# Relative-position biases of a two-block transformer: moved from the feed-forward stage into the set-up, with fewer, larger stores

## The chip, the core and the metric

The kernel runs on one core of a Trainium2 chip. The metric is the device time of one execution in microseconds; the time of a kernel is the median of its runs. TensorE is called PE, its weight loads PEld, VectorE DVE, ScalarE ACT, GpSimd POOL and SyncE SP. A "q" behind an engine's name stands for its instruction queue where it issues a transfer.

## The reference

Two blocks of two layers each on x (256 tokens x 1024, float32). The first block has, in each layer, a feed-forward part, three kinds of attention and a second feed-forward part, each behind a norm that is scaled and shifted by vectors made from a condition c. The change touches the biases of the sliding-window attention: a table of 32 buckets x 6 heads, looked up by the bucket of the distance between two positions.

```python
def modulate(x, g, shift, scale):
    return rms_norm(x, g) * (1.0 + scale[:, None, :]) + shift[:, None, :]
...
    cond = jax.nn.silu(c)
    for l in range(DEPTH):
        mod = cond @ w_mod[l] + b_mod[l]
        sh1, sc1, g1, sh2, sc2, g2, sh3, sc3, g3 = jnp.split(mod, 9, axis=-1)
        h = modulate(x, norm_g[l, 0], sh1, sc1)
        x = x + 0.5 * g1[:, None, :] * swiglu(h, w_ffn1_gu[l], w_ffn1_down[l])
...
def swa_attention(q, k, v, pos, sinks, rel_table):
...
    rel = pos.reshape(B, nb, WINDOW)[..., :, None] - band(pos)[..., None, :]
    bias = rel_table[t5_bucket(rel)].astype(jnp.float32)
```

The bias of a distance depends only on how many of 32 bucket edges the distance has reached, so it can be written as a sum of the table's steps over the edges reached.

## The kernel before

**Matmuls.** A float32 weight tile (`raw`, 128x1024, four 128-row chunks of 256 columns, 512 KB) is split into a high part (`whi`, ACT) and a low part (`wlo`, DVE); the operand likewise (`oph`, `opl`). A product is three matmuls: high x high (L218), low x high (L231), high x low (L235). PE runs its queue in order, as every engine does.

**The set-up** (`setup`) is a schedule written out by hand: the instructions go to the engines' queues in the order of the code. SP issues x in two halves, c, b_mod and norm_g, then the eight row blocks of w_mod for the scale vector "sc" (L437). PE transposes x (`take_x`, L771), ACT copies it to the chip and squares it, DVE adds the squares (`ssq`, L657, six adds). Then PE multiplies the condition by the eight row blocks (`gv`, L447, `self.next_step`). Behind the third of them it makes the row sums (L575), from which DVE takes the inverse root (`nv` ... `nry`, L584 to L540); behind the seventh it spreads them over the partitions (`dg`, L592 on DVE, L596 on PE). Then `fill_operand` makes `oph` and `opl` with the scale vector.

**The held products.** `held_parts` computes the first ten half blocks of `w_ffn1_gu` in the set-up, in a loop over b of 0 to 9. Block b is 24 matmuls. Behind an odd b below 8 DVE scales the two results (`held`, L351). Then come the steps of the shift vector "sh" (`gv`, as many as `SH_HELD` says), then `held.high(b + 2)` (ACT, L326) and `held.low(b + 2)` (DVE, L332): parts are made two blocks ahead. `LOADS` says what SP loads ahead of each block; one small load goes out with each letter.

**The biases.** `bias_loads` prepares ten small loads: `posk` (all positions to each partition), four of `posq`, four of the table, and `posi`. After block 5 (`REL_AT`) `rel_bias` makes `thr` (query position less edge, L1013, L1014), `kf` (key positions, L1016), the steps of the table (a matmul with `step`, L1018, then `tabs` and three bfloat16 parts `tabp`), and the first two of eight pieces `ge`: for four queries and 384 keys, whether each edge is reached (two instructions, L1035, on DVE). The rest is six "looks", each a function in the list `self.later`. A look is twelve bfloat16 matmuls (32 columns x 512, L1050) into one PSUM bank, one or two further pieces of `ge` (two buffers), an eviction `bev` by ACT (L1054) and four stores by ACT's queue (48 KB each, L1058), 24 stores in all, to `bias_scratch` in DRAM, which the attention reads much later.

**Behind the set-up.** In the feed-forward stage a framework schedules by priorities. `pace` pops one function of `self.later` at every third weight block (`T5_EVERY`) from the sixteenth (`T5_WAIT`): the six looks, then six functions `rest` (other vectors and the masks) and the rope tables. SP issues the stage's weight loads (L186) at the end of the set-up.

Of the kernel before, what the change touches and what calls it, by code (L numbers as in the profile page):

```python
# [9 lines left out]
F32 = mybir.dt.float32  # L10
F32R = mybir.dt.float32r
BF16 = mybir.dt.bfloat16
# [6 lines left out]
P = 128  # L19
# [26 lines left out]
SMALL = 1  # L46
LOADS = ("w", "sw", "sw", "sw", "sw", "ssw", "ssw", "w", "", "")
T5_HELD = (0,)*10
# [6 lines left out]
REL_AT = 5  # L55
# [76 lines left out]
class Net:  # L132
# [640 lines left out]
    def setup(self, tmp):  # L773
# [41 lines left out]
        with self.tc.manual_schedule():  # L815
# [12 lines left out]
            small_loads = self.bias_loads(tmp)  # L828
# [4 lines left out]
            nc.scalar.dma_start(early, A["cst"][:, o0:o1])  # L833
            self.x = self.t(self.xp, [P, 8, S], F32, "x")
# [5 lines left out]
            finish_1()  # L840
            for n in range(4):
                self.take_x(xn, n)
            self.preload(8)
            wgu, kp = A["w_ffn1_gu"][0], kept.enter_context(self.tc.tile_pool(name="kept", bufs=1))
# [20 lines left out]
            for b in range(10):  # L865
                for x in LOADS[b]:
# [5 lines left out]
                    for f in small_loads[:SMALL]:  # L872
                        f()
                    small_loads = small_loads[SMALL:]
# [22 lines left out]
        def rest(n):  # L897
# [12 lines left out]
            else:  # L910
                mk = self.t(tmp, [P, 512], F32, "bev", 2)
# [11 lines left out]
        self.later += [lambda n=n: rest(n) for n in range(6)] + [lambda: self.rope_tables(tmp)]  # L923
# [66 lines left out]
    def bias_loads(self, pool):  # L990
# [5 lines left out]
        self.posi = self.t(pool, [P, 2], I32, "posi")  # L996
        self.tab = self.t(pool, [P, 32], F32, "tab")
# [7 lines left out]
        pairs.append((self.posi, pos[0].rearrange("(t p) -> p t", p=P)))  # L1005
        return [lambda o=o, i=i: nc.sync.dma_start(o, i) for o, i in pairs]

    def rel_bias(self, pool):
        nc, A = self.nc, self.A
        self.scratch = nc.dram_tensor("bias_scratch", (6, P, 384), F32).ap()  # L1010
        posq, posk, tab = self.posq, self.posk, self.tab
        thr = self.t(pool, [P, 2, 32], F32, "thr")
        nc.vector.tensor_copy(thr, posq)  # L1013
        nc.vector.tensor_scalar(out=thr, in0=thr, scalar1=self.edges, scalar2=None, op0=ALU.subtract)  # L1014
        kf = self.t(pool, [P, S], F32, "kf")
        nc.vector.tensor_copy(kf, posk)  # L1016
        ps = self.sm()
        nc.tensor.matmul(ps[:, 0:32], lhsT=self.step, rhs=tab, start=True, stop=True)  # L1018
        steps = self.t(pool, [P, 32], F32, "tabs")
        nc.scalar.activation(out=steps, in_=ps[:, 0:32], func=AF.Copy)  # L1020
        parts, rest = [], steps
        for n in range(3):
            part = self.t(pool, [P, 32], BF16, "tabp%d" % n)
            nc.vector.tensor_copy(part, rest)
            parts.append(part)
            if n < 2:
                left = self.t(pool, [P, 32], F32, "tabr%d" % n)
                nc.vector.tensor_tensor(out=left, in0=rest, in1=part, op=ALU.subtract)
                rest = left
        ge = {}  # L1030

        def reached(piece):
            t = ge[piece] = self.t(pool, [P, 4, 384], BF16, "ge", 2)
            for a, w, blk in ((0, P, 0), (P, S, 1)):
                nc.vector.tensor_tensor(  # L1035
                    out=t[:, :, a : a + w],
# [4 lines left out]
        def look(n):  # L1041

            ps = self.sm()
            for t in range(4):
                piece, j = divmod(4 * n + t, 3)
                if piece not in ge:
                    reached(piece)
# [735 lines left out]
```

## Time and profile before

| | us |
|---|---|
| median of 3 runs | 1905.13 |
| lowest, highest run | 1897.05, 1905.39 |
| the profiled execution's own time | 1893.67 |
| its span | 1891.9 |
| mean granted clock over the span | 0.99 |

The span is the time from the first to the last instruction of the profiled execution. A row of a timeline gives start and length of a group of like instructions in us, the engine, line and operation, out<-in, and in brackets how long the engine was idle before it and what ended that. "PEclk" is the granted TensorE clock as a share of full speed.

### The profile page before, as it was taken

The numbers are of one execution on the slowest core, as the hardware profiler recorded it, in microseconds if no ns is written. First come the engines' busy times: TensorE is split into PE (matmuls) and PEld (weight loads), VectorE is DVE, ScalarE is ACT, GpSimd is POOL, SyncE is SP. The second block draws the span as 40 slices with busy tenths as digits, with TensorE's granted clock in tenths as the row PEclk, the third lists the DMA queues.
The fourth block names the chain that finished last, engine by engine and source line by source line (L and its number), as shares of the span: only waits on it lengthen the run. The fifth ranks groups of instructions, "written<-read, shape, count | busy, mean of one in ns | idle before, by whom it ended". The sixth has DMA issues, their size and how long they took to land.

```text
span 1891.9 us, 37147 instructions
## 1 busy us (share of the span) xinstructions
PE 1839.9 (97%) x15125; PEld 1736.0 (92%) x15125; DVE 1371.3 (72%) x2171; ACT 960.2 (51%) x1527; POOL 0.2 (0%) x4
## 2 busy tenths in 40 slices
PE   7999999999999999999999999999999999999998
PEld 5899996899999999968999988999999888999998
DVE  4897576698669765768986696679865777577554
ACT  3444475554445444756544454546444545455443
POOL 0000000000000000000000000000000000000000
PEclk8999999999999999999999999999999999999999
DMA  9698545789857963458798477578984585775550
GB/s 319 195 331 288 187 141 191 267 279 378 283 178 274 319 230 118 135 190 296 249 340 269 157 250 235 195 233 281 337 267 147 189 295 178 248 252 186 195 191 23
DMA packets 229447, 440.72 MB, mean 233 GB/s; under 512 B 15590, under 2 KB 79708, under 8 KB 229276
## 3 DMA queue, kind: packets, MB, share of 16 engines
q1 hardware_dynamic: 227740, 436.96, 68.0%
q8 instruction: 118, 1.93, 0.4%
q10 hardware_dynamic: 1536, 1.39, 0.2%
q14 instruction: 53, 0.43, 0.1%
HBM read 436.06 MB, written 2.23 MB: 232 GB/s over the span
## 4 chain that ended last, share of the span: by engine, by line
PE 87%; DVE 6%; DMA 3%; ACT 2%; issue 1%; SPq 0%; DVEq 0%; ACTq 0%
PE mm L218 24%; PE mm L235 23%; PE mm L231 23%; DVE wlo L198 2%; PE mm L262 2%; PE mm L265 2%; PE mm L263 2%; PE gv L447 2%; PE sm L771 1%; ACT whi L197 1%; DMA raw<-in_w_ffn_gu_dram 1%; PE mm L771 1%; PE gv L481 1%; DMA rawx<-in_w_mod_dram 1%; DMA raw<-in_w_mod_dram 1%
## 5 line engine op out<-in xcount | busy, mean ns | idle before, releaser
L218 PE MATMUL mm<-oph,whi 128*128 128x256 f32 (+1 forms) x3072 | 786.3, 282 | 13.3 <-DVE dly L302 4.9
L231 PE MATMUL mm<-opl,whi 128*128 128x256 f32 (+1 forms) x3072 | 780.0, 280 | 0.1
L197 ACT ACTIVATE whi<-raw 128x1024 fp32r<-128x1024 f32 (+2 forms) x408 | 426.2, 1047 | 455.4 <-PE mm L231 352.1
L198 DVE TENSOR_TENSOR wlo<-raw,whi 128x1024 fp32r<-128x1024 f32 (+2 forms) x408 | 489.8, 1208 | 176.5 <-ACT whi L197 168.5
L218 PEld LDWEIGHTS mm<-oph,whi 128*128 128x128 f32 x3072 | 582.5, 190 | 30.1 <-issue 10.3
L231 PEld LDWEIGHTS mm<-opl,whi 128*128 128x128 f32 x3072 | 582.6, 190 | 2.2 <-issue 0.9
L235 PE MATMUL mm<-oph,wlo 128*128 128x256 f32 (+1 forms) x3072 | 574.8, 280 | 8.6 <-DVE wlo L198 8.4
L235 PEld LDWEIGHTS mm<-oph,wlo 128*128 128x128 f32 x3072 | 453.9, 190 | 12.2 <-DVE wlo L198 11.1
L197 ACT ACTIVATE whi<-rawx 128x1024 fp32r<-128x1024 f32 x160 | 170.1, 1064 | 193.8 <-PE mm L231 159.0
L218 PE MATMUL mm<-ah,whi 128*128 128x256 f32 x1056 | 268.1, 278 | 0.0
L231 PE MATMUL mm<-al,whi 128*128 128x256 f32 x1056 | 267.0, 277 | 0.0
L198 DVE TENSOR_TENSOR wlo<-rawx,whi 128x1024 fp32r<-128x1024 f32 x160 | 194.8, 1223 | 91.3 <-ACT whi L197 90.6
L454 DVE SCALAR_TENSOR_TENSOR acc<-raw,silc,acc 128x1024 f32<-128x1024 f32 x119 | 152.5, 1283 | 77.9 <-DMA raw<-in_w_ada_dram 60.4
L235 PE MATMUL mm<-ah,wlo 128*128 128x256 f32 x1056 | 206.8, 277 | 0.7 <-DVE wlo L198 0.7
L218 PEld LDWEIGHTS mm<-ah,whi 128*128 128x128 f32 x1056 | 198.4, 188 | 3.0 <-issue 2.5
L231 PEld LDWEIGHTS mm<-al,whi 128*128 128x128 f32 x1056 | 198.5, 188 | 0.0
L235 PEld LDWEIGHTS mm<-ah,wlo 128*128 128x128 f32 x1056 | 159.5, 188 | 1.1 <-DVE wlo L198 1.1
L262 PE MATMUL mm<-whi,oph 128*128 128x512 f32 (+2 forms) x192 | 73.9, 388 | 0.3 <-ACT oph L640 0.2
L263 PE MATMUL mm<-whi,opl 128*128 128x512 f32 (+2 forms) x192 | 73.0, 380 | 0.0
L454 DVE SCALAR_TENSOR_TENSOR acc<-rawx,silc,acc 128x1024 f32<-128x1024 f32 x42 | 53.9, 1283 | 18.3 <-DMA rawx<-in_w_ada_dram 9.3
L698 ACT ACTIVATE ah<-sil 128x512 fp32r<-128x512 f32 x66 | 40.3, 624 | 37.0 <-DVE sil L760 29.7
L265 PE MATMUL mm<-wlo,oph 128*128 128x512 f32 (+2 forms) x192 | 56.6, 378 | 0.0
(374 smaller groups left out, 1660.3 us busy)
## 6 DMA issues: line engine op xcount, KB each, us to landing
raw<-in_w_mod_dram SPq DMA_DIRECT2D x119, 512.0 KB
raw<-in_w_ffn_gu_dram SPq DMA_DIRECT2D x104, 512.0 KB
raw<-in_w_in_dram SPq DMA_DIRECT2D x104, 512.0 KB
raw<-in_w_ada_dram SPq DMA_DIRECT2D x75, 512.0 KB
rawx<-in_w_ffn_gu_dram SPq DMA_DIRECT2D x64, 512.0 KB
raw<-in_w_ffn_down_dram SPq DMA_DIRECT2D x54, 512.0 KB
raw<-in_w_ffn_in_dram SPq DMA_DIRECT2D x48, 512.0 KB
rawx<-in_w_ffn_in_dram SPq DMA_DIRECT2D x40, 512.0 KB
```

The source lines that it names most:

```text
L197: nc.scalar.activation(out=whi[:, :tot], in_=src, func=AF.Copy)
L198: nc.vector.tensor_tensor(out=wlo[:, :tot], in0=src, in1=whi[:, :tot].bitcast(F32), op=ALU.subtract)
L218: i0 = nc.tensor.matmul(o, lhsT=whi[:, k, cs], rhs=xhi[:, kop0 + k, :ncol], start=zero and (opener or not shared), stop=False, **kw)
L231: nc.tensor.matmul(o, lhsT=whi[:, k, cs], rhs=xlo[:, kop0 + k, :ncol], start=False, stop=False, **kw)
L235: nc.tensor.matmul(o, lhsT=wlo[:, k, cs], rhs=xhi[:, kop0 + k, :ncol], start=False, stop=last and k == nk - 1, **kw)
L262: nc.tensor.matmul(o, lhsT=xhi[:, kop0 + k, ts], rhs=whi[:, k, cols], start=first and k == 0, stop=False)
L263: nc.tensor.matmul(o, lhsT=xlo[:, kop0 + k, ts], rhs=whi[:, k, cols], start=False, stop=False)
L265: nc.tensor.matmul(o, lhsT=xhi[:, kop0 + k, ts], rhs=wlo[:, k, cols], start=False, stop=last and k == nk - 1)
L447: nc.tensor.matmul(acc[32 * g : 32 * g + 32, 0:S], lhsT=self.cond[cond][1][:, k, :], rhs=row[:, g * S : (g + 1) * S], start=k == 0, stop=k ...
L454: nc.vector.scalar_tensor_tensor(out=acc, in0=row, scalar=self.cond[cond][0][:, k : k + 1], in1=acc, op0=ALU.mult, op1=ALU.add)
L698: nc.scalar.activation(out=hi, in_=src, func=AF.Copy)
L771: self.nc.tensor.transpose(out, in_, self.ident[:n, :n])
```

## The change

The small loads go to ACT's queue at the very start, nine of them; the table is loaded once per group of 32 partitions into `buckets` and copied into a matmul operand by four DVE copies. `thr`, `kf` and `ge` 0 and 1 stand among the x steps, the step-table matmul ahead of the first `gv`; two looks stand among the row blocks of the scale vector, four in the loop of the held products, each further piece behind `held.low`. The six evictions are kept in six buffers, and SP stores them, 256 KB each, at the end of the loop, with two unused heads as padding (8 heads in `bias_scratch`). `self.later` holds only the six `rest` and the rope tables. The mask's staging tile has a buffer of its own.

```diff
-SMALL = 1
-T5_HELD = (0,)*10
+LOOK_AT = (3, 5)
-REL_AT = 5
...
-            small_loads = self.bias_loads(tmp)
+            self.posi = self.t(tmp, [P, 2], I32, "posi")
+            kp = kept.enter_context(self.tc.tile_pool(name="kept", bufs=1))
...
             nc.scalar.dma_start(early, A["cst"][:, o0:o1])
+            self.bias_loads(kp)
+            bias = self.rel_bias(kp)
...
             finish_1()
+            bias.distances()
+            bias.reached(0)
             for n in range(4):
                 self.take_x(xn, n)
+                if n == 1:
+                    bias.reached(1)
+            bias.table()
             self.preload(8)
...
                 if n == RS_AT:
                     rs = self.row_rs(self.mm)
+                if n == LOOK_AT[0]:
+                    bias.look(0)
+                    bias.reached(2)
+                if n == LOOK_AT[1]:
+                    bias.look(1)
+                    bias.reached(3)
                 if n == RB_AT:
                     self.rb = self.row_scale(self.mm, rs)
...
                     held.high(b + 2)
                     held.low(b + 2)
-                if b == REL_AT:
-                    self.later = self.rel_bias(tmp)
-                for _ in range(T5_HELD[b]):
-                    self.later.pop(0)()
+                if b == 1:
+                    bias.look(2)
+                if 2 <= b <= 5:
+                    bias.reached(b + 2)
+                if 3 <= b <= 5:
+                    bias.look(b)
+            nc.sync.dma_start(self.posi, A["positions"][0].rearrange("(t p) -> p t", p=P))
+            for _ in range(6):
+                bias.store()
...
-                mk = self.t(tmp, [P, 512], F32, "bev", 2)
+                mk = self.t(tmp, [P, 512], F32, "mk")
...
-        self.later += [lambda n=n: rest(n) for n in range(6)] + [lambda: self.rope_tables(tmp)]
+        self.later = [lambda n=n: rest(n) for n in range(6)] + [lambda: self.rope_tables(tmp)]
...
-            pairs.append((self.tab[rows, 6 * g : 6 * g + 6], A["rel_bias"]))
+            pairs.append((self.buckets[rows], A["rel_bias"]))
+        for o, i in pairs:
+            nc.scalar.dma_start(o, i)
...
+            def table(self):
+
+                for g in range(4):
+                    rows = slice(32 * g, 32 * g + 32)
+                    nc.vector.tensor_copy(net.tab[rows, 0:6, g], net.buckets[rows])
+                ps = net.sm()
+                nc.tensor.matmul(
+                    ps[:, 0:32], lhsT=net.step, rhs=net.tab.rearrange("p h g -> p (h g)"), start=True, stop=True
+                )
...
+                ev = net.t(pool, [P, 512], F32, "bev", 6)
+                nc.scalar.activation(out=ev, in_=ps, func=AF.Copy)
+                evs.append((n, ev))
+
+            def store(self):
+                n, ev = evs.pop(0)
+                to = net.scratch.rearrange("h (g r) k -> (h g) (r k)", g=4)[:, 2048 * n : 2048 * n + 2048]
+                nc.sync.dma_start(to.rearrange("m (t c) -> t m c", t=4), ev)
```

In the changed kernel lines up to some 820 are 2 lower than before (L447 is L445, L332 is L330, L351 is L349, L575 is L573, L596 is L594, L657 is L655); the looks' matmuls are at L1073, `ge` at L1060, the step-table matmul at L1043, the stores at L1081.

In the rows of order below, a number behind a name only tells buffers apart.

PE between the transposes of x (`mm<-ident`) and the fourth row block of the scale vector, before:

```order
L771 MATMUL mm_153<-ident_75,raw_77 128x128
L771 MATMUL mm_153<-ident_75,raw_78 128x128
L447 MATMUL gv_181<-raw_100,repc_112 32x256 x4
L447 MATMUL gv_181<-raw_102,repc_112 32x256 x4
L447 MATMUL gv_181<-raw_104,repc_112 32x256 x4
L575 MATMUL mm_195<-ones_81,ssq_124 128x1 x2
L575 MATMUL mm_195<-ones_81,sq_162 128x1 x2
L447 MATMUL gv_181<-raw_164,repc_112 32x256 x4
```

and after:

```order
L769 MATMUL mm_177<-ident_75,raw_77 128x128
L769 MATMUL mm_177<-ident_75,raw_78 128x128
L1043 MATMUL sm_192<-tab_99,cst_4_80 128x32
L445 MATMUL gv_220<-raw_115,repc_127 32x256 x4
L445 MATMUL gv_220<-raw_117,repc_127 32x256 x4
L445 MATMUL gv_220<-raw_119,repc_127 32x256 x4
L573 MATMUL mm_234<-ones_81,ssq_145 128x1 x2
L573 MATMUL mm_234<-ones_81,sq_186 128x1 x2
L445 MATMUL gv_220<-raw_206,repc_127 32x256 x4
L1073 LDWEIGHTS tabp_44_196
L1073 MATMUL sm_263<-ge_136,tabp_44_196 32x512
```

The step-table matmul `sm<-tab,cst` now stands between the transposes and the first `gv`. The first look's matmuls (`sm<-ge,tabp`, 24 rows with their weight loads) follow the fourth row block, the second look's follow the sixth, ahead of `L594`.

DVE in the same place, from the last two of the six adds of squares into the steps of the inverse root, before:

```order
L657 TENSOR_TENSOR ssq_124<-ssq_124,sq_150 128x256
L657 TENSOR_TENSOR ssq_124<-ssq_124,sq_159 128x256
L584 TENSOR_SCALAR nv_194<-mm_195 128x2
L513 TENSOR_SCALAR nri_201<-nv_194 128x2
L515 TENSOR_SCALAR nry_203<-nri_201 128x2
L521 TENSOR_SCALAR nrh_206<-nv_194 128x2
L536 TENSOR_SCALAR nrt_205<-nry_203,nrh_206 128x1 x2
```

and after, from `kf` to the four copies:

```order
L1035 CAST kf_111<-posk_97 128x256
L1060 TENSOR_TENSOR ge_136<-thr_110,kf_111 128x4x128
L1060 TENSOR_TENSOR ge_136<-thr_110,kf_111 128x4x256
L655 TENSOR_TENSOR ssq_145<-ssq_145,sq_147 128x256
L655 TENSOR_TENSOR ssq_145<-ssq_145,sq_156 128x256
L655 TENSOR_TENSOR ssq_145<-ssq_145,sq_159 128x256
L1060 TENSOR_TENSOR ge_162<-thr_110,kf_111 128x4x128
L1060 TENSOR_TENSOR ge_162<-thr_110,kf_111 128x4x256
L655 TENSOR_TENSOR ssq_145<-ssq_145,sq_171 128x256
L655 TENSOR_TENSOR ssq_145<-ssq_145,sq_174 128x256
L655 TENSOR_TENSOR ssq_145<-ssq_145,sq_183 128x256
L1041 COPY tab_99<-tabl_98 32x6 x4
```

`thr` (just above), `kf` and a piece of `ge` stand ahead of the first add, a second piece between the third and the fourth add, and four copies of the table behind the sixth. Of `ge` 2 and 3, four rows stand further on, between the last step of the root and `dg`.

DVE in the loop of held products, from the low part for block 4 to that for block 7, before:

```order
L332 TENSOR_TENSOR wlo_392<-kept_358,whi_390 128x1024
L351 TENSOR_TENSOR held_424<-mm_361,rb_241 128x256 x2
L332 TENSOR_TENSOR wlo_433<-kept_397,whi_431 128x1024
L332 TENSOR_TENSOR wlo_472<-kept_438,whi_470 128x1024
L351 TENSOR_TENSOR held_505<-mm_441,rb_241 128x256 x2
L332 TENSOR_TENSOR wlo_518<-kept_479,whi_516 128x1024
```

and after:

```order
L330 TENSOR_TENSOR wlo_477<-kept_444,whi_475 128x1024
L1060 TENSOR_TENSOR ge_479<-thr_110,kf_111 128x4x128
L1060 TENSOR_TENSOR ge_479<-thr_110,kf_111 128x4x256
L349 TENSOR_TENSOR held_510<-mm_446,rb_316 128x256 x2
L330 TENSOR_TENSOR wlo_519<-kept_484,whi_517 128x1024
L1060 TENSOR_TENSOR ge_521<-thr_110,kf_111 128x4x128
L1060 TENSOR_TENSOR ge_521<-thr_110,kf_111 128x4x256
L330 TENSOR_TENSOR wlo_574<-kept_541,whi_572 128x1024
L1060 TENSOR_TENSOR ge_576<-thr_110,kf_111 128x4x128
L1060 TENSOR_TENSOR ge_576<-thr_110,kf_111 128x4x256
L349 TENSOR_TENSOR held_624<-mm_543,rb_316 128x256 x2
L330 TENSOR_TENSOR wlo_637<-kept_598,whi_635 128x1024
```

Each `ge` (pieces 4 to 7) is behind the low part of two blocks ahead. For pieces 5 and 7 a held product and a low part stand ahead of it.

## Rows read from the trace of the kernel before

**Rows 1.** The page, busy time and share of the span of each engine.

```profile
PE 1839.9 (97%) x15125; PEld 1736.0 (92%) x15125; DVE 1371.3 (72%) x2171; ACT 960.2 (51%) x1527; POOL 0.2 (0%) x4
```

**Rows 2.** Windows: us, busy us (x instructions) of five engines, PEclk, DMA share, GB/s.

```profile
10.80:24.00 13.20, 9.46 (x80) 3.76 (x79) 5.21 (x26) 4.80 (x12) 0.00 (x0) 0.74 0.97 331
24.00:61.40 37.40, 36.21 (x309) 32.12 (x310) 23.52 (x43) 12.81 (x20) 0.00 (x0) 0.95 0.81 276
61.40:182.00 120.60, 117.99 (x1055) 109.98 (x1054) 109.76 (x159) 63.16 (x93) 0.00 (x0) 1.00 0.82 278
```

**Rows 3.** PE's waits from 61.4 to 250 us: total us, times, longest us.

```profile
PE mm L218 <- ACT dlc L301: 1.1, 1, 1.1
```

**Rows 4.** Timeline of PE, 9 to 24 us: start, length, what, [idle before].

```profile
10.77 1.90 PE L447 MATMUL gv<-raw,repc 128*32 128x256 f32 x24
...
13.59 0.61 PE L575 MATMUL mm<-ones,ssq 128*128 128x1 f32 x4 [0.92 <-DVE ssq L657]
...
19.64 1.22 PE L596 MATMUL mm<-dg,ones 128*128 128x256 f32 x2
20.79 1.08 PE L447 MATMUL gv<-raw,repc 128*32 128x256 f32 x8
```

**Rows 5.** Timeline of DVE, 7 to 24 us.

```profile
7.46 0.28 DVE L796 COPY rw1T<-mm 128x120 f32<-128x120 f32 x1 [1.36 <-PE mm L771]
...
10.63 0.95 DVE L657 TENSOR_TENSOR ssq<-ssq,sq 128x256 f32<-128x256 f32 x2 [0.51 <-ACT sq L655]
...
14.68 0.16 DVE L584 TENSOR_SCALAR nv<-mm 128x2 f32<-128x2 f32 x1 [1.14 <-PE mm L575]
...
17.20 0.47 DVE L592 TENSOR_SCALAR dg<-ident,nry 128x128 f32<-128x128 f32 x2
```

**Rows 6.** Timeline of ACT, 0 to 8 us, the issues.

```profile
0.74 0.41 ACTq L817 DMA_DIRECT2D ident<-in_cst_dram  x1
```

**Rows 7.** The chain that ended last, 180 to 300 us: start, length, what.

```profile
182.36 6.90 DMA bev<-in_cst_dram
```

**Rows 8.** Timeline of DVE, 38 to 56 us.

```profile
39.02 0.76 DVE L351 TENSOR_TENSOR held<-mm,rb 128x256 f32<-128x256 f32 x2 [3.74 <-PE mm L235]
39.69 2.35 DVE L332 TENSOR_TENSOR wlo<-kept,whi 128x1024 fp32r<-128x1024 f32 x2
...
47.82 0.19 DVE L1013 CAST thr<-posq 128x64 f32<-128x64 int32 x1
...
48.21 0.29 DVE L1016 CAST kf<-posk 128x256 f32<-128x256 int32 x1
...
49.39 3.56 DVE L1035 TENSOR_TENSOR ge<-thr,kf 128x512 bf16<-128x512 f32 x4
```

**Rows 9.** Timeline of PE, 39 to 43.5 us, two blocks' first matmuls.

```profile
39.48 0.39 PE L218 MATMUL mm<-oph,whi 128*128 128x256 f32 x1
...
42.98 0.39 PE L218 MATMUL mm<-oph,whi 128*128 128x256 f32 x1
```

**Rows 10.** Timeline of PE, 161.2 to 163 us, one look.

```profile
161.74 0.85 PE L1050 MATMUL sm<-ge,tabp 128*32 128x512 bf16 x12
```

**Rows 11.** Timeline of ACT, 142 to 148 us, one eviction and its four issues.

```profile
142.94 0.59 ACT L1054 ACTIVATE bev<-sm 128x512 f32<-128x512 f32 x1
143.56 2.53 ACTq L1058 DMA_DIRECT2D bias_scratch<-bev  x4
```

**Rows 12.** Timeline of ACT, 62 to 68 us, the stage's first weight.

```profile
65.80 1.05 ACT L197 ACTIVATE whi<-raw 128x1024 fp32r<-128x1024 f32 x1
```

**Rows 13.** Windows of 4 us, columns as in rows 2.

```profile
400.00:404.00 4.00, 2.00 (x15) 1.59 (x13) 4.00 (x9) 2.53 (x6) 0.00 (x0) 1.00 0.74 239
404.00:408.00 4.00, 3.98 (x20) 3.98 (x21) 4.00 (x5) 0.00 (x0) 0.00 (x0) 0.57 0.62 196
```

**Rows 14.** Timeline of SP, 46 to 60 us, the five issues.

```profile
46.61 7.87 SPq L186 DMA_DIRECT2D raw<-in_w_ffn_gu_dram  x5
```

**Rows 15.** DMA view, 142 to 156 us: the queue's packets, MB, share of 16 engines.

```profile
q10 hardware_dynamic: 112, 0.20, 3.7%
```

More of the change, by code (lines that the diff above doesn't have):

```diff
@@ L840, in setup @@
             finish_1()
+            bias.distances()
+            bias.reached(0)
             for n in range(4):
                 self.take_x(xn, n)
+                if n == 1:
+                    bias.reached(1)
+            bias.table()
             self.preload(8)
-            wgu, kp = A["w_ffn1_gu"][0], kept.enter_context(self.tc.tile_pool(name="kept", bufs=1))
+            wgu = A["w_ffn1_gu"][0]
             held = self.held_parts(tmp, kp, wgu, (0, DFF, S, DFF + S, 2 * S))
@@ L871, in setup @@
                         nw += 1
-                    for f in small_loads[:SMALL]:
-                        f()
-                    small_loads = small_loads[SMALL:]
                 held.matmuls(b)
@@ L995, in bias_loads @@
         self.posk = self.t(pool, [P, S], I32, "posk")
-        self.posi = self.t(pool, [P, 2], I32, "posi")
-        self.tab = self.t(pool, [P, 32], F32, "tab")
+        self.buckets = self.t(pool, [P, 6], F32, "tabl")
+        self.tab = self.t(pool, [P, 8, 4], F32, "tab")
         nc.vector.memset(self.tab, 0.0)
@@ L1003, in bias_loads @@
             pairs.append((self.posq[rows], quarters[g].partition_broadcast(32)))
-            pairs.append((self.tab[rows, 6 * g : 6 * g + 6], A["rel_bias"]))
-        pairs.append((self.posi, pos[0].rearrange("(t p) -> p t", p=P)))
-        return [lambda o=o, i=i: nc.sync.dma_start(o, i) for o, i in pairs]
+            pairs.append((self.buckets[rows], A["rel_bias"]))
+        for o, i in pairs:
+            nc.scalar.dma_start(o, i)
     def rel_bias(self, pool):
-        nc, A = self.nc, self.A
@@ L1010, in rel_bias @@
-        self.scratch = nc.dram_tensor("bias_scratch", (6, P, 384), F32).ap()
-        posq, posk, tab = self.posq, self.posk, self.tab
+        nc = self.nc
+        net = self
+        self.scratch = nc.dram_tensor("bias_scratch", (8, P, 384), F32).ap()
+        parts, ge, evs = [], {}, []
         thr = self.t(pool, [P, 2, 32], F32, "thr")
-        nc.vector.tensor_copy(thr, posq)
-        nc.vector.tensor_scalar(out=thr, in0=thr, scalar1=self.edges, scalar2=None, op0=ALU.subtract)
         kf = self.t(pool, [P, S], F32, "kf")
-        nc.vector.tensor_copy(kf, posk)
@@ L1017, in rel_bias @@
[L1017 to L1036, printed above, removed]
-                    in0=thr[:, blk, 4 * piece : 4 * piece + 4].unsqueeze(2).to_broadcast([P, 4, w]),
-                    in1=kf[:, 0:w].unsqueeze(1).to_broadcast([P, 4, w]), op=ALU.is_ge,
-                )
[L1041 to L1047, printed above, removed]
-                src = ge[piece].rearrange("p a b -> p (a b)")[:, j * 512 : (j + 1) * 512]
-                for m, part in enumerate(parts):
-                    nc.tensor.matmul(ps[32 * t : 32 * t + 32, :], lhsT=part, rhs=src, start=m == 0, stop=m == 2)
-            if n < 5:
-                reached((4 * n + 6) // 3)
-            ev = self.t(pool, [P, 512], F32, "bev", 2)
-            nc.scalar.activation(out=ev, in_=ps, func=AF.Copy)
-            rows = self.scratch.rearrange("h (g i q) k -> i g h (q k)", g=4, q=4)
-            for t in range(4):
-                piece, j = divmod(4 * n + t, 3)
-                nc.scalar.dma_start(rows[piece, :, :, j * 512 : (j + 1) * 512], ev[32 * t : 32 * t + 24, :])
@@ L1064, in rope_tables @@
+        return Bias()
     def rope_tables(self, pool):
```

32 lines of the change are left out of this document (29 added, 3 removed).

## The prediction

> **What bounds the kernel now.** I read the page's busy times first. TensorE (PE) is busy 97% of the span [rows 1], so a change pays only if it takes work or a wait off PE, and it costs whatever wait it puts there. Next I read the busy times by stage, since that 97% is a mean. In the stretch of the held products PE is busy 36.21 of 37.40 us, and in the part of the feed-forward stage that holds the looks 117.99 of 120.60 [rows 2]. One stretch differs: from 10.8 to 24 us PE is busy 9.46 of 13.20 us, the DMA engines are at a share of 0.97, and the granted clock is 0.74 of full speed. PE waits for modulation weights there, DVE is busy 5.21 us and ACT 4.80. So the set-up has spare time on DVE before 24 us, and none on PE after it. The waits of PE in the feed-forward stage tell how much the old place of the biases costs beyond its own matmuls: the longest group of waits there is 1.1 us in total and belongs to another tile [rows 3]. The old place therefore costs PE the looks themselves and little else.
>
> **The load stretch.** Now every DVE step of the biases that stands ahead of PE's first vector matmul must be counted, because the step-table matmul (one, 32 columns) is now ahead of gv on PE's in-order queue, and it needs the table copies, which stand behind two `ge` pieces and all the sum-of-squares adds on DVE. Before, gv begins at 10.77 and its last row block begins at 20.79 and takes 1.08, so it ends at 21.87 [rows 4]. After:
>
> - Start of `thr`. DVE is free at 7.74, after rw1T [rows 5]. The four posq loads are issued on ACT's queue, nine small loads of about 0.41 each [rows 6] behind two others, so the fourth posq leaves at about 4.9. How long it takes to land is not shown for this moment. The longest small load that I found takes 6.90 [rows 7]; that gives 11.8. Bounds 7.74 and 11.8; the engines are nearly full at this time, so neither end is out, and I take 9.5, about the middle.
> - `thr` and `kf` run from 47.82 to 48.50 before, 0.68 in all; four `ge` instructions (two pieces) take 3.56, so a piece is 1.78 [rows 8]. Two adds take 0.95 [rows 5], so six take 2.85. The four table copies are not in the trace. Their nearest row is the 0.19 cast of 128x64 [rows 8]; nothing excludes 0.1 or 0.3 each; I take 0.2, 0.8 together.
> - So the matmul of the step table comes at 9.5 + 0.68 + 1.78 + 1.43 + 1.78 + 1.42 + 0.8 = 17.4, and gv begins at about 17.7, not at 10.77. Its 6.9 us of lateness are not all lost, since before gv itself waited for loads. Those will have landed: before, the last row block's arrive by 20.8.
> - From there: three row blocks 1.90, row sums 1.1 (13.59 to 14.68), rsqrt steps 2.5 (14.68 to 17.20) [rows 4, 5], which is 23.2. DVE then does `ge` piece 2 (1.78), PE the second look, which needs it (its last half, about 0.4), DVE piece 3 (1.78) and only then the two `dg` (0.47), for which L596 on PE waits: 27.6. L596 is 1.15 up to the next row and the last gv 1.08 [rows 4], at a reduced clock as before; at full clock both halve. That ends at 28.7 to 29.8 against 21.87.
>
> I take **+7**; with `thr` at 7.74 and full clock it is +4, with `thr` at 11.8 and half clock +10. The two looks and row sums that lie inside cost PE nothing more: it waits for DVE there anyway. The weight loads 6 and 7, whose buffers gv 0 and 1 set free, go out some 6 us later too; they still land ahead of 27.
>
> **The held loop.** Call T the end of block 3. Before, DVE does the held product (0.76 for both halves) and then the low parts (2.35 for two, so 1.17 each) [rows 8], and PE doesn't wait, for it runs a block ahead: block and vector step take 3.50 (39.48 to 42.98) [rows 9]. After, `ge` piece 5 stands behind held product 3 and low part 5 on DVE, and look 3 on PE, right behind block 3, ends with three matmuls on that piece. So PE waits until T + 0.7 + 1.17 + 1.78 = T + 3.65, and block 4 starts at T + 4.1 instead of T + 0.46: **+3.65**. Look 2 is ready in time and costs its own 0.75 to 0.85 [rows 10]. Behind look 3 ACT evicts (0.59 [rows 11]), makes high part 6 (1.05 [rows 12]), DVE low part 6 (1.17) and piece 6 (1.78), which look 4 needs: T + 8.7, its last half done at T + 9.1. Block 4 with its vector step is done at T + 7.5: **+1.6**. Block 5 again has a held product ahead of low part 7 and piece 7 (0.7 + 1.17 + 1.78), and nine of look 5's matmuls need piece 7; the vector steps there (two, some 1.1) cover part: 3.65 + 0.65 of matmuls - 1.1 = 3.2, less the old step-table matmuls' 0.25: **+2.9**. Sum 0.75 + 3.65 + 1.6 + 2.9 = **+8.9**. If DVE were free in time, only four looks would remain, 4 x 0.85 less 0.25, about +3. A wait chain longer by an eviction each time gives +10.
>
> **The clock.** From 400 to 404 us PE is busy 2.00 of 4, and in the next 4 us the granted clock is 0.57 instead of 1.00 [rows 13]. That is some 1.7 us lost (0.43 of 4). Block 3's and block 5's waits are 2.5 us or longer, so two such dips could come, 3.4 us. The first may overlap look 4's wait. I take **+2**, bounds 0 and +3.4.
>
> **The feed-forward stage.** It loses six looks of 0.85 [rows 10], 5.1. The first may lie in the norm's wait, giving 4.3. I take **-5.1**. ACT sheds six evictions of 0.59 and 24 issues (four take 2.53) [rows 11], some 19 us; DVE sheds six pieces, some 11. PE's waits there hardly depend on either [rows 3]: **-0.5**, at most the whole 2.6 us that PE is idle in that window [rows 2], at least nothing. Against it, the mask load now goes out next to its use and can stall DVE like the 6.90 of [rows 7]; PE lost little by that.
>
> **What is hidden.** The six stores (256 KB each) and the posi load stand on SP behind the held loads and ahead of the five weight loads that SP issues from 46.61 [rows 14], and these wait for the sixth store's issue, so for look 5's eviction. The first of those weights is used at 65.80, when ACT makes its high part [rows 12], 19 us after that issue. A 2 KB packet of the old stores takes 0.037 x 16 x 14 us / 112 = 74 ns [rows 15]; six stores are 768 packets, 57 engine-us, 3.6 us over 16 engines. That fits in the 19 us: nothing. The last tile in the kept buffers is freed by these stores, before the stage's silu needs the room.
>
> The Trainium skill ("DMA: Bandwidth & Descriptors", section "Why a DMA increments its semaphore by 16 and not by 1") says that a transfer issued by an engine's own queue uses only as many DMA engines as divide the slowest dimension of both its sides. The stores' slowest dimension is 4, so by that rule four engines carry them. No row here shows how many engines a store uses.
>
> **Sum:** 7 + 8.9 + 2 - 5.1 - 0.5 = +12.3, about +12. The profiled execution took 1893.67 us, so it would become 1906; the runs' median is 1905.13, 11.5 above it, with runs from 1897 to 1905, and the same +12 gives 1917. Half a per cent, 9.5 us, is about what a measurement of this kernel can tell from no change.
>
> **Rivals.**
> *The waits are covered.* `thr` starts at 7.74 and the `ge` pieces overtake nothing that PE needs: 4 + 3 + 0 - 5.1 - 0.5 = +1.4, at best 4 + 3 - 5.1 - 2.6 = -0.7: about 1906. For it: DVE idles 14 of 37.4 us in the held stretch [rows 2]. Against: the idle time lies ahead of each held product, and the pieces behind it. Chance 0.3, with what lies between it and the forecast.
> *The other side, DVE and ACT relief.* PE's waits and clock later in the first block fall with 19 us less of ACT's queue and 11 of DVE's, because weight splits come earlier, and raw buffers with them. It decides if PE's idle 2.6 us in that window and the set-up's bound are both at their ends, and the transferred wait vanishes: 0 + 3 - 5.1 - 2.6 = -4.7, 1900; to be faster by 9.5 it must also gain in later stages, which the rows don't promise. Chance 0.1, with 0.04 for more than 9.5.
> *All upper ends.* posq late, half clock, both dips: 10 + 10 + 3.4 - 5.1 = +18, 1923. Chance 0.15.
> *A tail of stores.* Should the stores run on four of the 16 engines, 57 engine-us are 14.2 us, and the five loads behind them end on those four last. Counted from block 6's start the stores leave at 1, and the first load lands at 1 + 14.2 + some 3 of its own, 18 us, about when it is needed (19). Missing it costs some 3 us on top: +15, 1920. The page's rule on engines told above would bring this about. Chance 0.08.
> That the looks stay where they were is excluded by the order of the built program: they stand among the row blocks and the blocks.
>
> **How the numbers follow.** The forecast has 0.37, the rivals 0.3, 0.1, 0.15 and 0.08. Slower by over 9.5: most of the forecast (0.33), the two dearer rivals (0.23), together 0.56; faster 0.04; the rest 0.40. The range leaves out the second rival and the upper edge: 1902 to 1926.
>
> **What would show it.** gv begins at 16 to 19 us, and the last one ends at 27 to 30. In the held stretch PE waits for `ge` three times, some 2.5, 1 and 2 us; the first block of the stage starts some 16 us later. The stage from there to the same block is 4 to 6 us shorter. No wait of PE on the raw loads after the stores. I am wrong if gv begins before 14, or if PE waits for `ge` less than 3 us in the held stretch, or if times far into the kernel shift by more than 3 us.

## The result and the profile after

The changed kernel takes 1916.11 us (median of 7 runs, 1912.24 to 1929.21) against 1899.45 us of the kernel before in the same rounds: ratio 1.0081, interval 1.006 to 1.0101, so slower by 11 to 19 us. Two further measurements of the same kernel gave 1.007 (1.0049 to 1.009) and 1.0084 (1.0056 to 1.0113).

The profiled execution of the changed kernel took 1924.09 us, 8 above the median; that of the kernel before took 1893.67, 6 below its median. So the difference of the two profiled spans (30.4 us) is more than the change's. The program's order behind the first feed-forward stage is the same in both kernels. So the two traces are compared at one instruction near the stage's end, the 73rd high part of a weight on ACT:

```profile
250.63 0.88 ACT L197 ACTIVATE whi<-raw 128x832 fp32r<-128x832 f32 x1
...
268.83 0.89 ACT L195 ACTIVATE whi<-raw 128x832 fp32r<-128x832 f32 x1
```

It starts at 250.63 us before and at 268.83 after, 18.2 us later. In the two further measurements of the changed kernel it stands at 266.22 and 265.12. The part behind it lasted between 1641 and 1654 us in the fourteen profiled executions of this study, with no pattern that an edit explains; the shortest is the kernel before's. A difference of some 3 us between two single traces can be chance: block 0, the first of the held products, starts at 23.99 us in the kernel before and at 21.47 in run 8 below, whose code up to there is the same.

The page of the changed kernel, its span and busy times:

```profile
span 1922.3 us, 37133 instructions
...
PE 1847.4 (96%) x15125; PEld 1744.9 (91%) x15125; DVE 1372.5 (71%) x2175; ACT 960.3 (50%) x1527; POOL 0.2 (0%) x4
```

PE's busy time is 7.5 us above that of [rows 1]; most of the span's growth is waits. The windows of the changed kernel, columns as in [rows 2], cut at its own stages: two pieces of the load stretch, the held products, the stage up to 200 us.

```profile
10.80:24.00 13.20, 7.52 (x71) 4.84 (x74) 8.75 (x29) 4.78 (x13) 0.00 (x0) 0.74 0.72 274
24.00:33.90 9.90, 5.74 (x46) 2.62 (x38) 5.38 (x17) 3.33 (x7) 0.00 (x0) 0.74 1.01 350
33.90:81.60 47.70, 41.53 (x356) 34.53 (x356) 25.79 (x39) 14.56 (x23) 0.00 (x0) 0.95 0.60 196
81.60:200.00 118.40, 111.54 (x975) 108.23 (x974) 100.87 (x154) 59.71 (x87) 0.00 (x0) 0.97 0.83 283
```

The held products now take 47.7 us, and PE is idle for 6.2 of them (before: 1.2 of 37.4). The stage from 81.6 to 200 has 6.9 us without PE; before it was 2.6 of 120.6 [rows 2].

The load stretch on PE, start, length, what, [idle before]. Block 0 of the kernel before stands first:

```profile
23.99 0.39 PE L218 MATMUL mm<-oph,whi 128*128 128x256 f32 x1 [1.00 <-ACT oph L701]
```

```profile
17.91 0.63 PE L1043 MATMUL sm<-tab,cst 128*128 128x32 f32 x2 [5.68 <-DVE tab L1041]
18.47 2.79 PE L445 MATMUL gv<-raw,repc 128*32 128x256 f32 x24
...
21.19 0.90 PE L573 MATMUL mm<-ones,ssq 128*128 128x1 f32 x4
...
22.47 0.64 PE L445 MATMUL gv<-raw,repc 128*32 128x256 f32 x8
...
29.19 1.19 PE L594 MATMUL mm<-dg,ones 128*128 128x256 f32 x2 [0.96 <-DVE dg L590]
30.31 1.08 PE L445 MATMUL gv<-raw,repc 128*32 128x256 f32 x8
...
33.91 0.58 PE L216 MATMUL mm<-oph,whi 128*128 128x256 f32 x1 [1.00 <-ACT oph L699]
```

These answer to [rows 4]: `gv` starts at 18.47 instead of 10.77, behind the step-table matmul that waited 5.68 us for DVE's table copies; the last `gv` ends at 31.39 instead of 21.87; block 0 starts at 33.91, before at 23.99, 9.9 us later. DVE shows why:

```profile
9.73 0.29 DVE L804 COPY repc<-silc 128x256 f32<-128x256 f32 x1 [4.05 <-ACT silc L802]
9.94 0.28 DVE L794 COPY rw1T<-mm 128x120 f32<-128x120 f32 x1
10.14 0.18 DVE L1033 CAST thr<-posq 128x64 f32<-128x64 int32 x1
...
10.84 1.83 DVE L1060 TENSOR_TENSOR ge<-thr,kf 128x512 bf16<-128x512 f32 x2
12.59 1.48 DVE L655 TENSOR_TENSOR ssq<-ssq,sq 128x256 f32<-128x256 f32 x3
13.98 1.82 DVE L1060 TENSOR_TENSOR ge<-thr,kf 128x512 bf16<-128x512 f32 x2
...
17.11 0.74 DVE L1041 COPY tab<-tabl 32x6 f32<-32x6 f32 x4
...
25.10 3.55 DVE L1060 TENSOR_TENSOR ge<-thr,kf 128x512 bf16<-128x512 f32 x4
28.57 0.47 DVE L590 TENSOR_SCALAR dg<-ident,nry 128x128 f32<-128x128 f32 x2
```

The queue runs nearly without a gap from `thr` at 10.14 to the copies at 17.11, and `dg` at 28.57 stands behind 3.55 us of `ge`. `thr` itself comes right behind two copies of the set-up that were late: `rw1T` (9.94, before 7.46 [rows 5]), and ahead of it `repc`, which waited for `silc` on ACT. ACT makes `silc` at 9.49 (before 5.57), since its queue first issues the nine small loads and only then loads the table of the function:

```profile
8.20 1.28 ACT L802 ACT_TABLE_LOAD   x1 [8.20 <-DMA posq<-in_positions_dram]
```

`rw1T` also needs norm_g from SP's queue, whose transpose on PE came at 8.86 instead of 6.99; the transposes of x behind it began at 9.09 instead of 7.22. SP's waits up to 36 us, total, times, longest:

```profile
SPq L787 <- DMA posk<-in_positions_dram: 4.7, 1, 4.7
```

That is the issue of b_mod (L787), held for 4.7 us until posk, a load of ACT's queue, had landed. It went out at 6.70 instead of 1.98, the first row block of w_mod at 7.45 instead of 2.82.

The granted clock has a part in the load stretch too. This is the window of the 24 `gv`, columns as in [rows 2]:

```profile
18.47:21.26 2.79, 2.79 (x26) 1.06 (x25) 0.93 (x5) 0.20 (x1) 0.00 (x0) 0.50 0.22 48
```

Behind its wait of 5.68 us PE runs them at 0.50, the lower of the two levels (1.2 GHz). What that costs shows in the rows above: eight `gv` take 1.08 us at 30.31, where the clock is 0.50 (28.7 to 38.9 us), and 0.64 at 22.47, where it is 1.00.

The held loop on PE at the looks behind blocks 3, 4 and 5:

```profile
50.17 0.82 PE L1073 MATMUL sm<-ge,tabp 128*32 128x512 bf16 x9
53.49 0.81 PE L1073 MATMUL sm<-ge,tabp 128*32 128x512 bf16 x3 [2.50 <-DVE ge L1060]
54.23 0.38 PE L216 MATMUL mm<-oph,whi 128*128 128x256 f32 x1
...
58.93 0.83 PE L1073 MATMUL sm<-ge,tabp 128*32 128x512 bf16 x6 [0.51 <-DVE ge L1060]
59.69 0.38 PE L216 MATMUL mm<-oph,whi 128*128 128x256 f32 x1
...
66.42 0.84 PE L1073 MATMUL sm<-ge,tabp 128*32 128x512 bf16 x9 [2.09 <-DVE ge L1060]
67.19 0.38 PE L216 MATMUL mm<-oph,whi 128*128 128x256 f32 x1
```

From one block's first matmul to the next it was 3.50 [rows 9], and 4.18 from block 5 (42.98) to block 6, which has two vector steps ahead of it and the old step-table matmul:

```profile
47.16 0.36 PE L218 MATMUL mm<-oph,whi 128*128 128x256 f32 x1
```

Now it is 7.45 from block 3 to 4 (46.78 to 54.23), 5.46 to block 5 and 7.50 to block 6. PE's waits in the feed-forward stage behind it:

```profile
PE mm L233 <- DVE wlo L196: 2.6, 1, 2.6
PE mm L216 <- ACT dlc L299: 1.7, 1, 1.7
PE mm L216 <- ACT whi L195: 1.6, 2, 1.1
```

The first two fall at 106 to 112 us, and the granted clock dips there (0.50 from 110.6 to 117.4 us): it is 0.97 in the window to 200 us, where it was 1.00.

### The profile page after: what moved, and what is told of

Read it like the earlier page. It is cut to its first block, busy times and chain, and to the rows that moved or that the text cites. A ratio compares the mean times of both kernels' runs of the same rounds, so it can differ in the third digit from the quotient of the medians.

```text
span 1922.3 us, 37133 instructions
## 1 busy us (share of the span) xinstructions
PE 1847.4 (96%) x15125; PEld 1744.9 (91%) x15125; DVE 1372.5 (71%) x2175; ACT 960.3 (50%) x1527; POOL 0.2 (0%) x4
## 4 chain that ended last, share of the span: by engine, by line
PE 82%; DVE 8%; DMA 5%; ACT 2%; issue 2%; ACTq 0%; DVEq 0%; SPq 0%
PE mm L216 23%; PE mm L233 22%; PE mm L229 22%; DVE wlo L196 3%; PE gv L445 2%; PE mm L260 2%; PE mm L263 2%; PE mm L261 2%; DMA raw<-in_w_ada_dram 2%; DMA rawx<-in_w_ada_dram 1%; ACT whi L195 1%; PE sm L769 1%; DMA raw<-in_w_mod_dram 1%; DVE acc L452 1%; DMA raw<-in_w_ffn_gu_dram 1%
## 5 line engine op out<-in xcount | busy, mean ns | idle before, releaser
L233 PE MATMUL mm<-oph,wlo 128*128 128x256 f32 (+1 forms) x3072 | 578.2, 282 | 14.6 <-DVE wlo L196 14.5
L233 PEld LDWEIGHTS mm<-oph,wlo 128*128 128x128 f32 x3072 | 457.2, 191 | 18.2 <-DVE wlo L196 17.2
L233 PE MATMUL mm<-ah,wlo 128*128 128x256 f32 x1056 | 206.8, 277 | 0.0
L233 PEld LDWEIGHTS mm<-ah,wlo 128*128 128x128 f32 x1056 | 159.4, 188 | 0.5 <-DVE wlo L196 0.4
L696 ACT ACTIVATE ah<-sil 128x512 fp32r<-128x512 f32 x66 | 40.2, 624 | 39.1 <-DVE sil L758 32.7
```

Of the source, the lines that this page charges most:

```text
L233: nc.tensor.matmul(o, lhsT=wlo[:, k, cs], rhs=xhi[:, kop0 + k, :ncol], start=False, stop=last and k == nk - 1, **kw)
L696: nc.scalar.activation(out=hi, in_=src, func=AF.Copy)
```

## The experiments

"First block" is the start of block 0, "mark" the 73rd high part; before they stand at 23.99 and 250.63, in the changed kernel at 33.91 and 268.83. Ratios are against the kernel before on the same chip. Runs 1 to 4 shared one chip, 5 to 8 another, 9 to 12 a third.

**Run 1, the early loads alone.**

```diff
 nc.scalar.dma_start(early, A["cst"][:, o0:o1])
+for o, i in small_loads[:9]:
+    nc.scalar.dma_start(o, i)
...
```

> The kernel before with one edit: the nine small loads go out on ACT's queue at the start, as in the change; everything else of the biases stays where it was. Theory 1 (the set-up is late because DVE's steps of the biases stand ahead of PE's first gv): gv starts near 10.8 and block 0 near 24, the time stays within 3 us of the kernel before. Rival 1 (the nine loads themselves hold up SP's loads, as b_mod's issue at 6.70 instead of 1.98 in the changed kernel hints): the first w_mod issue is again near 7.4, gv starts 3 to 5 us later, block 0 near 28.5, the time is 4 to 5 us above the kernel before.

Ratio 1.0006 (0.9987 to 1.0024). SP's issue again waited for posk, and `gv` and block 0 began late (SP's wait; two rows of PE's timeline):

```profile
SPq L789 <- DMA posk<-in_positions_dram: 4.5, 1, 4.5
```

```profile
12.57 2.54 PE L447 MATMUL gv<-raw,repc 128*32 128x256 f32 x24
...
25.74 0.58 PE L218 MATMUL mm<-oph,whi 128*128 128x256 f32 x1 [1.00 <-ACT oph L701]
```

So rival 1's mechanism is there: the first w_mod issue is 4.4 us later (7.25 for 2.82). ACT's `silc` is late as well (9.29 for 5.57). But `gv` starts only 1.8 us later, block 0 1.75 and the mark 3.0 (253.58), no more than single traces differ by chance, and nothing reaches the time. Rival 1's 3 to 5 us at `gv` and its block 0 near 28.5 did not come.

**Run 2, the load stretch in another order.**

```diff
-            bias.table()
             self.preload(8)
...
-                if n == LOOK_AT[0]:
-                    bias.look(0)
-                    bias.reached(2)
-                if n == LOOK_AT[1]:
-                    bias.look(1)
-                    bias.reached(3)
+                if n == 5:
+                    bias.table()
                 if n == RB_AT:
                     self.rb = self.row_scale(self.mm, rs)
+                    bias.reached(2)
+                if n == 7:
+                    bias.look(0)
+                    bias.look(1)
...
             held.low(1)
+            bias.reached(3)
...
-                t = ge[piece] = net.t(pool, [P, 4, 384], BF16, "ge", 2)
+                t = ge[piece] = net.t(pool, [P, 4, 384], BF16, "ge", 3)
```

> The changed kernel with the load stretch in another order: the table's step matmul behind the sixth gv, looks 0 and 1 behind the last gv, piece 2 of ge behind dg, piece 3 behind the low part of block 1 (three buffers for ge). The early loads and pieces 0 and 1 stay. Theory 1: gv no longer waits for DVE and block 0 starts at 25 to 27 instead of 33.9; the time falls by 7 to 9 us against the changed kernel, to about 1908. Rival 1 (the loads are late): gv starts only when the weights land, block 0 at 28 to 31, the time falls by 3 to 6.

First block 28.52, mark 261.81, so 5.4 and 7.0 us earlier than in the changed kernel. Block 0 is in rival 1's range (28 to 31), not in theory 1's. What is left shows on PE: the row sums wait for adds that stand behind two pieces of `ge`.

```profile
12.81 2.48 PE L445 MATMUL gv<-raw,repc 128*32 128x256 f32 x24
17.23 0.61 PE L573 MATMUL mm<-ones,ssq 128*128 128x1 f32 x4 [1.95 <-DVE ssq L655]
```

The time didn't follow: ratio 1.0083 (1.0061 to 1.0105), as the changed kernel's. Run 11 takes this up.

**Run 3, the pieces of the held loop ahead.**

```diff
-                if 2 <= b <= 5:
-                    bias.reached(b + 2)
-                if 3 <= b <= 5:
-                    bias.look(b)
+                if b in (2, 4):
+                    bias.reached(b + 2)
+                    bias.reached(b + 3)
+                if b == 3:
+                    bias.look(3)
+                if b == 5:
+                    bias.look(4)
+                    bias.look(5)
...
```

> The changed kernel with pieces 4 and 5 of ge behind the low part for block 4, and 6 and 7 behind the low part for block 6, so that none stands behind a held product and a low part that PE waits for next; looks 4 and 5 stand together behind block 5; three buffers for ge. Theory 1 (the waits are DVE's order alone, and DVE has idle time ahead of each held product): PE's waits for ge of 2.5, 0.5 and 2.1 us in the loop go, block 0 to block 6 takes 26 to 27 us instead of 33.3, the time falls by 6 to 8 us to about 1909. Rival (DVE is short of time there and the wait moves to low parts or held products): less than 3 us are gained.

No wait of PE for `ge` is left in the loop. From block 0 to the shift vector's last step (L494) it takes 32.1 us (33.47 to 65.59), in the changed kernel 40.2 (33.91 to 74.06), before 30.0: 8 of the 10 us are gone. What stays, 2.1, is near four looks less the old step-table matmul: with look 3 between them, block 3 to block 4 now takes 4.15 us (45.84 to 49.98), so a look that waits for nothing adds 0.65 to 3.50. Look 3 runs in one piece:

```profile
49.22 0.83 PE L1077 MATMUL sm<-ge,tabp 128*32 128x512 bf16 x12
```

Mark 257.64, 11 us earlier; ratio 1.005 (1.0032 to 1.0069), which is some 4 to 6 us less than the changed kernel's 1.007 to 1.0084 on other chips. So theory 1's mechanism holds: the waits came from DVE's order alone. In the time the gain is at or below the 6 to 8 us that it expected, at the mark above it.

**Run 4, the stores on ACT's queue.**

```diff
-            for _ in range(6):
-                bias.store()
...
                 evs.append((n, ev))
+                self.store()
...
-                nc.sync.dma_start(to.rearrange("m (t c) -> t m c", t=4), ev)
+                nc.scalar.dma_start(to.rearrange("m (t c) -> t m c", t=4), ev)
```

> The changed kernel with each of the six stores on ACT's queue right behind its eviction, not on SP ahead of the stage's five weight loads. Rival 2 (the stores hold up those loads, and PE's waits of 1.7 and 2.6 us at 106 to 112 us with the clock's dip behind them come from it): the five loads go out some 8 to 10 us earlier, those waits go, the time falls by 4 to 6 us. Theory 1 (the stores are hidden): the weights land earlier but the time stays within 2 us of the changed kernel.

The five weight loads went out 4.8 us earlier, and the wait stayed:

```profile
63.73 12.53 SPq L184 DMA_DIRECT2D raw<-in_w_ffn_gu_dram  x5
```

```profile
PE mm L233 <- DVE wlo L196: 2.9, 1, 2.9
```

Mark 268.49, as in the changed kernel. The loop is 2 us longer, now that ACT issues in it (33.74 to 75.98), the stage behind it 180.7 us (87.78 to 268.49), as in the other profiles of the change (183.0, 181.2, 180.0). So the stores' place on SP's queue doesn't delay the stage. The ratio, 1.0131 (1.0103 to 1.0158), was worse than either expected; see run 12.

**Run 5, the changed kernel again.**

> The changed kernel without an edit, so that the others of this round, and runs 2 to 4, have it beside the same kernel before. If the kernel's shift by 250 us (18 us) is the change's cost and what differs behind it is chance, the ratio is again near 1.008; if chance made the first runs too good, it is nearer 1.012 and runs 2 and 3 did gain.

Ratio 1.007 (1.0049 to 1.009), mark 266.22. So chance had not made the first runs too good.

**Run 6, runs 2 and 3 together** (both diffs).

> Runs 2 and 3 together: the load stretch and the held loop both in the other order. Theory 1 (the two delays are separate and add): at 250 us it stands 18 - 7 - 11 = 0 to 2 us behind the kernel before, the time is 0 to 5 us above it. Rival (what one order saves the other wait takes back): the shift at 250 us stays above 5 us.

Ratio 1.0017 (0.9997 to 1.0038), first block 28.80, mark 253.31, 2.7 us behind the kernel before, a little more than theory 1's 0 to 2 and less than its rival's 5. The interval and that of run 5, the changed kernel on the same chip, don't meet: the two orders make most of the slowdown. The two gains nearly add: 4.8 of the 9.9 us are left ahead of block 0, 2.1 of the 10.2 us in the loop, and the stage takes back 4.

**Run 7, two small loads.** The query positions come out of posk, the table is loaded once.

```diff
-        for g in range(4):
-            rows = slice(32 * g, 32 * g + 32)
-            pairs.append((self.posq[rows], quarters[g].partition_broadcast(32)))
-            pairs.append((self.buckets[rows], A["rel_bias"]))
...
+        nc.scalar.dma_start(self.posk, pos[0].partition_broadcast(P))
+        nc.scalar.dma_start(self.buckets[0:32], A["rel_bias"])
...
```

> Run 6 with two small loads in place of nine: posk, and the table once for 32 partitions; the query positions are cast out of posk in four pieces, the table's copies read the one load. Theory 3 (each transfer takes the next of eight completion counters in turn and waits for the transfer that had it last, so nine small loads between them hold up SP's b_mod load until posk has landed): b_mod and the first w_mod go out before 4 us again and block 0 starts 1 to 3 us earlier than in run 6. Rival (the queue is held by the engines' load): SP's issues stay at 6 us or later, block 0 as in run 6.

```profile
1.98 0.40 SPq L787 DMA_DIRECT2D rows<-in_b_mod_dram  x1
5.39 0.32 SPq L787 DMA_DIRECT2D rows<-in_norm_g_dram  x1
```

b_mod is out at 1.98 as before; norm_g, the next, now waits, for `ident`, until 5.39, and the first w_mod goes out at 5.76, not before 4. So theory 3 holds for b_mod alone: with fewer loads the wait moves to the next transfer in turn. First block 27.54, 1.3 us earlier than in run 6; that is less than the same set-up code gives by chance (28.52, 28.80 and 30.98 in runs 2, 6 and 11). ACT's queue is free earlier here too (`silc` at 6.18), so the run doesn't price SP's wait by itself. Ratio 1.0016 (0.9994 to 1.0038), as run 6.

**Run 8, the kernel before without looks in the stage.** It leaves out the biases: its 24 stores write zeros.

```diff
-            ps = self.sm()
...
-            ev = self.t(pool, [P, 512], F32, "bev", 2)
-            nc.scalar.activation(out=ev, in_=ps, func=AF.Copy)
+            ev = blank
...
+        nc.vector.memset(blank, 0.0)
```

> The kernel before without the looks' matmuls, evictions and later pieces of ge; the 24 stores write a blank tile, so the window attention's biases are zeros. Theory 1 (a look costs PE its 0.85 us wherever it stands): the stage is 5 us shorter at 250 us, the time 4 to 6 us below the kernel before. Rival 3 (PE waits for weights at the same places instead, as at 106 to 112 us in the changed kernel): 2 us or less are gained.

Ratio 0.9986 (0.9972 to 1.0001), a gain of 2.7 us at the middle that is not clear of none. From the stage's first high part to the mark it takes 187.1 us (66.56 to 253.65), with the looks 184.8 (65.80 to 250.63). PE, with some 5 us less to do, waits instead (61 to 250 us):

```profile
PE mm L235 <- DVE wlo L198: 6.2, 8, 1.6
PE mm L218 <- ACT whi L197: 2.7, 2, 1.5
```

Before, these two groups were 1.1 and 0.2 us. The time lies between theory 1 and rival 3; the trace has rival 3's waits: the looks filled time in which weight parts were late. The 24 stores stay in this kernel, so whether loads or ACT's issues make the parts late isn't told apart.

**Run 9, the kernel before with six stores.**

```diff
...
-            for t in range(4):
-                piece, j = divmod(4 * n + t, 3)
-                nc.scalar.dma_start(rows[piece, :, :, j * 512 : (j + 1) * 512], ev[32 * t : 32 * t + 24, :])
+            to = self.scratch.rearrange("h (g r) k -> (h g) (r k)", g=4)[:, 2048 * n : 2048 * n + 2048]
+            nc.scalar.dma_start(to.rearrange("m (t c) -> t m c", t=4), ev)
```

> The kernel before with the change's table layout and its six stores of 256 KB, one behind each look on ACT's queue, in place of 24; the biases stay where they were. If the merged stores matter by themselves, ACT's queue is 11 us shorter in the stage and PE's waits there (2.8 us in all) shrink: 1 to 3 us are gained. If only the move matters, or four engines make a store slow, the time is within 2 us of the kernel before or a little above it.

Ratio 1.0045 (1.0032 to 1.0058), against both. Two waits make it. The four table copies, which the six stores' layout needs, stood behind DVE's other work, ahead of a matmul on PE's queue (timeline of PE, then windows behind it):

```profile
49.90 0.64 PE L1022 MATMUL sm<-tab,cst 128*128 128x32 f32 x2 [2.20 <-DVE tab L1020]
```

```profile
46.00:50.00 4.00, 1.80 (x24) 1.02 (x22) 3.02 (x10) 0.00 (x0) 0.00 (x0) 0.98 0.66 200
50.00:56.00 6.00, 6.00 (x45) 5.29 (x46) 4.40 (x9) 0.44 (x2) 0.00 (x0) 0.73 0.30 103
```

That is 2.2 us and a clock of 0.73 for 6 us. Near 198 us DVE waited 8.48 us for the mask's load, which shares a buffer with the evictions (the chain that ended last, 175 to 206 us):

```profile
185.17 8.14 DMA bias_scratch<-bev
...
193.33 7.20 DMA bev<-in_cst_dram
```

The last store took 8.14 us to land, the load behind it 7.20; PE stood still for some 3.5. So the run doesn't tell what merged stores cost by themselves; in the changed kernel the mask has a buffer of its own. It does price table copies on DVE ahead of a matmul of PE, which the changed kernel has too.

**Runs 10 to 12, the kernels of the change, of run 2 and of run 4 on one chip.**

> The changed kernel once more, as the mark for runs 11 and 12 on the same chip: ratio 1.007 to 1.008, 16 to 18 us behind at 250 us.

> Run 2 once more, now beside the changed kernel on one chip. Run 2 gained 7 us up to 250 us and nothing in the time, against the changed kernel's runs on another chip. If the two chips made that difference, it is now 4 to 8 us below run 10; if the gain is lost behind 250 us, it is again within 3 us of run 10.

> Run 4 once more, beside the changed kernel on one chip. If the stores on ACT's queue cost nothing, as the equal shift at 250 us says, it is within 3 us of run 10; if its ratio of 1.013 was the stores', it is 8 to 10 us above run 10.

Ratios 1.0084 (1.0056 to 1.0113), 1.0064 (1.005 to 1.0078), 1.0071 (1.0053 to 1.009); medians 1921.04, 1916.82 and 1917.58. Run 10's mark is 14.5 us behind the kernel before, less than the 16 to 18 expected. Run 11 is 4 us below run 10, with its block 0 2.6 us earlier (30.98 against 33.60) and its mark 1.7 (263.43 against 265.12): the gain of that order alone is small, 2 to 7 us at the mark and 0 to 4 in the time, where the intervals of runs 10 and 11 overlap. Run 12 is within 4 us of run 10 in the time; its mark, 269.41, is 4.3 later, with the longer loop of run 4 (33.00 to 75.55). The 1.0131 of run 4 did not come back.

## Why the prediction was right, and where its terms were not

The sign, the size (12 forecast; 11 to 19 measured, 9 to 17 in run 5) and the two places were right. By its own steps:

- **The load stretch, +7: it was +9.9.** The chain's times came near (`thr` at 10.14 for 9.5, the step-table matmul at 17.91 for 17.4), but the first by luck. The forecast let `thr` wait for its loads, between 7.74, when "DVE is free", and 11.8. (The 6.90 us in that upper end belong to the mask's 256 KB tile, no small load.) `thr` did not wait for them: DVE came to it only at 10.1, since norm_g and ACT's `silc` were late. What the sum had not at all is that ACT's small loads hold SP's loads and ACT's own next work; it looked at the queue, not at what the transfers share. Run 1 has both, and its block 0 is 1.75 us later. The step that was too small is "three row blocks 1.90, row sums 1.1": from the first `gv` to `nv` it took 4.1 us (18.47 to 22.58), for 3.0, at a granted clock of 0.50 for the `gv`. In run 10 it was 4.6, at the lower level too (see the end of this document). "Those will have landed" held.
- **The held loop, +8.9: it was +10.2** (40.2 against 30.0). Each wait came where it was put: 2.5 us behind block 3, 0.5 behind 4, 2.1 behind 5. Run 3 takes away 8 us by order alone.
- **The clock, +2: not there.** The waits of 2.5 and 2.1 us in the loop left no dip; the clock is 0.95 in that stretch as before [rows 2]. What the lower level did cost lies in the load stretch, where the forecast had it among its bounds. A dip came at 110.6 us, in a wait that the forecast didn't have.
- **The stage, -5.6: it was -1.9 to -4.8** (from its first high part to the mark 183.0, 181.2 and 180.0 us in the three profiles, before 184.8). This step failed: "it loses six looks of 0.85". The 0.85 of [rows 10] is too much, for the next matmul starts 0.78 us after the look's first (161.74 to 162.52). And without the looks PE meets late weight parts, 2.4 to 2.6 us at L233 in all three profiles. Run 8 leaves out the looks and gains 2.7 us at the middle, where no gain is not excluded.
- **Hidden stores: right in the price.** Off SP's queue they made the stage no shorter (runs 4 and 12). But the 3.6 us over 16 engines were wrong: the stores were slow. The DMA view of 58 to 70 us shows mostly two tenths of the 16 engines busy from about 61 us, and from 64 to 69 us, where little but the stores moves, the share of SP's queue is 26.3%, 4.2 engines:

```profile
DMA  0015799995312261312222312222222222222226
...
q1 hardware_dynamic: 251, 0.50, 26.3%
```

The Trainium skill ("DMA: Bandwidth & Descriptors", section "Why a DMA increments its semaphore by 16 and not by 1") gives four engines for such a transfer, whose slowest dimension is 4 on one side; the trace agrees. Three of the weight loads behind the stores waited for stores to land, 7.5 us in all (SP's waits from 58 to 90 us):

```profile
SPq L184 <- DMA bias_scratch<-bev: 7.5, 3, 3.0
```

So the rival of the stores' tail was right that they are slow and wrong in the price: in run 4 those loads went out 4.8 us earlier and the stage gained nothing.

Sum of what was measured at the mark: 9.9 + 10.2 - 1.9 = 18.2 for this profile, 14.5 for run 10. The ratio's 11 to 19 us agree. That the forecast's total came within 5 us is in part luck: its 2 us for dips in the loop, which did not come, made good some of what the load stretch and the loop cost beyond it, while its relief in the stage was too large.

Of its signs, `gv` at 18.47 and the three waits for `ge` fell as said; the last `gv` ended at 31.39 (27 to 30 said), and the stage began 20.1 us later (16 said). By one sign it would be wrong: "if times far into the kernel shift by more than 3 us". Behind the mark the three traces of the changed kernel are 12.2, 3.6 and 4.1 us longer than the one trace before. They differ by 8.7 us among themselves, so whether the change costs something there stays open.

No kernel here beats the one before clear of chance. Run 6 comes back to it, and run 8 bounds what could be won by putting the looks elsewhere, with the 24 stores left where they are: 0.28% at most.

## What to carry to other kernels

Work that is moved into an engine's idle time is free only behind what the bottleneck waits for next: the loop with the pieces of `ge` and four looks cost 10 us with each piece behind the low part, and 2 with them ahead of the held products. Before taking work out of a stage, ask whether the bottleneck would only wait there; six looks of 0.85 us were worth 2.7 at the middle, not 5. A transfer moved to another queue still shares something with those that stay, and it holds up its new engine's own work: look at SP's waits for transfers that aren't SP's, and at what stands behind the issues on ACT.

## What the runs showed beyond this

Small loads on ACT's queue held SP's issue until one of them had landed, 4.7 us here, 4.5 in run 1; in the trace each issue takes one of eight counters and waits for the transfer that had it last. With two loads instead of nine the wait passed to norm_g.

A granted clock of 1.00 in a window is only as good as the records under it. The windows of run 10 show 1.00 from 10.8 us on, but the first clock record of its trace stands at 27.3 us. Eight `gv` took 1.08 us ahead of it (at 22.84) and 0.64 behind it (at 30.85), so the clock was at its lower level there as in the changed kernel's first trace: the length of a like matmul told the level.
